# More feed-forward buffers, tail splits on GpSimd, and six other edits to a two-layer encoder step on one core

## The chip, the cores and the metric

The kernel runs on one core of a Trainium2 chip. The metric is the time of one execution on the device in microseconds, the median of several runs. The engines go by the profile's names: PE is TensorE (matmuls; PEld are its weight loads), DVE is VectorE, ACT is ScalarE, POOL is GpSimd, and SP is SyncE, which here only issues DMAs.

## The reference, cut to what matters

One step of a two-layer encoder (`D_MODEL` 1024, feed-forward width 2816) for 1024 prompt frames and 32 sample frames, in float32. Layer 0 mixes with a matrix-memory recurrence over 8 heads, layer 1 with windowed attention. Each mixer and each feed-forward is followed by a layer norm.

```python
def swiglu(x, w_gu, w_down):
    g, u = jnp.split(x @ w_gu, 2, axis=-1)
    return (jax.nn.silu(g) * u) @ w_down

def mlstm_chunk(q, k, v, ig, lf, C0, n0, m0):
    ...
    qk = jnp.einsum('bhtd,bhsd->bhts', q, k) * d
    num = w_inter[..., None] * jnp.einsum('bhtd,bhde->bhte', q, C0) + jnp.einsum('bhts,bhse->bhte', qk, v)
    ...
    C_new = decay[..., None, None] * C0 + jnp.einsum('bhs,bhsd,bhse->bhde', w_end, k, v)

def trunk(x, ...):
    for layer in range(DEPTH):
        ...  # mix: recurrence with w_in_a, w_out_a, or attention with w_kv, w_q_b, w_out_b
        x = layer_norm(DEEPNORM_ALPHA * x + mix, ln_g[layer, 0], ln_b[layer, 0])
        x = layer_norm(DEEPNORM_ALPHA * x + swiglu(x, w_gu[layer], w_down[layer]), ln_g[layer, 1], ln_b[layer, 1])
```

Outputs are the two sets of frames, the recurrence's states and the last keys and values.

## The kernel before

**Data and splits.** Prompt and sample frames stand side by side as 1056 columns; the 1024 features lie in 8 tiles of 128 partitions. Every large matmul is made from three matmuls in a reduced float format: each operand is split into a high half (a cast on ACT) and a low half (the difference), and `gemm` (L361 to L363) adds high x high, high x low and low x high. The activations' halves are the tile `SX`, made by `split_act` (ACT L391, DVE L392).

**Weights.** The class `Weights` brings 512 KB pieces from memory into three raw buffers (`wr`) and makes their halves in order, two jobs for a unit: the cast on ACT (L201), the low half on POOL, or on DVE for keys in `on_vector` (both L203). Five slots (`wh`, `wl`) hold the products; some jobs have a home of their own elsewhere (`W.home`, shown as `ex`, `oh`). Down projections of pairs use sums and differences of weight quarters (seven products instead of eight, L174 to L180 on DVE). A raw buffer is loaded anew when its last job is done.

**Order.** The order of instructions is fixed while the program is built. `gemm` calls `wv.tick` with the estimated PE time after each step, and `Weave` then lets background tasks (norms, staging of feed-forward results, feeding of loads) issue their next piece. Engines run their queues in order, so an instruction that waits holds those behind it.

**Stages.** First q, k, v of the recurrence: frames in three column groups, head pairs j = 0 to 3. The recurrence runs as a background pipeline per pair and chunk of 128 frames; chunk c = 8 is the sample, with 32 rows, and its tiles are cut to `[:L]`. `scores`, `values` and `place` hold its matmuls (L886 to L953). Then the mixer's output and its norm by quarters of 264 columns, and the feed-forward: `up_tile` makes hidden tiles with PSUM tags `A` and `B` of two buffers each; results lie in `Z` buffers from the list `free` (six of eleven), and `stage` splits pairs of them through buffers 7 to 10 and stores them (L1269 to L1271). `alloc` drains the oldest staging task when `free` is empty. The last tile runs `behind` after each product, which loads blocks for the down projection. `down` adds into `act` (L1465, L1467).

**Tail.** The last block of the down projection runs by quarters and output tiles (eight units, L1520 to L1525), with five PSUM banks in a ring, and after each quarter a norm task `ln_task`. The very last quarter of the kernel has a class of its own, `LastNorm`, which sums while the products come and ends with the variance, the scaling and the stores (L549 to L587).

```python
            if final and g == 3:
                wv.drain(tasks[1])
                run(g, cols, None, LastNorm(box[0].z, box[0].lnps, QUARTERS[g], li))
```

## Time and profile before

| | |
|---|---|
| median of 3 runs | 2239.36 us (2236.99 to 2242.18) |
| the profiled execution | 2235.46 us, span 2233.7 us |
| granted TensorE clock | 0.996 |
| busy: PE, DVE, ACT, POOL | 2184.5, 1465.8, 998.1, 1035.1 us |
| moved by DMA | 298.10 MB |

The span runs from the first to the last instruction of the profiled execution. A row of the timeline gives the start in us, the length in us, the engine, the line of the kernel, the operation, what it writes and reads, its shape and count, and in brackets the engine's idle time before it and what ended it. Two matmuls in a row overlap, so their lengths add up to more than the time that they hold PE; starts are what counts.

### The profile page before, as it was taken

The numbers are of one execution on the slowest core, as the hardware profiler recorded it, in microseconds if no ns is written. First come the engines' busy times: TensorE is split into PE (matmuls) and PEld (weight loads), VectorE is DVE, ScalarE is ACT, GpSimd is POOL, SyncE is SP. The second block draws the span as 40 slices with busy tenths as digits, with TensorE's granted clock in tenths as the row PEclk, the third lists the DMA queues.
The fourth block names the chain that finished last, engine by engine and source line by source line (L and its number), as shares of the span: only waits on it lengthen the run. The fifth ranks groups of instructions, "written<-read, shape, count | busy, mean of one in ns | idle before, by whom it ended". The sixth has DMA issues, their size and how long they took to land.

```text
span 2233.7 us, 44246 instructions
## 1 busy us (share of the span) xinstructions
PE 2184.5 (98%) x17086; PEld 2147.9 (96%) x17086; DVE 1465.8 (66%) x2848; ACT 998.1 (45%) x2253; POOL 1035.1 (46%) x977
## 2 busy tenths in 40 slices
PE   9999999999999999999999999999999999999997
PEld 9899989999999999999998999899999999999997
DVE  4465577777566565566667778788565666456657
ACT  4443355455444444322236778756444444332124
POOL 2544331003666666544316776600566666554422
PEclk9999999999999999999999999999999999999998
DMA  4222112211433443697426433411344434397712
GB/s 150 74 55 67 48 44 87 98 39 58 164 137 143 154 145 143 217 331 237 159 78 179 114 99 96 152 65 39 116 152 158 143 130 152 135 353 240 256 50 79
DMA packets 174499, 298.10 MB, mean 133 GB/s; under 512 B 18064, under 2 KB 130760, under 8 KB 174288
## 3 DMA queue, kind: packets, MB, share of 16 engines
q1 hardware_dynamic: 169936, 290.94, 39.0%
q10 hardware_dynamic: 4352, 4.33, 0.6%
q8 instruction: 135, 2.21, 0.4%
q14 instruction: 76, 0.62, 0.1%
HBM read 201.80 MB, written 82.94 MB: 127 GB/s over the span
## 4 chain that ended last, share of the span: by engine, by line
PE 77%; DVE 9%; ACT 5%; DMA 3%; issue 3%; POOL 2%; SPq 0%; ACTq 0%; POOLq 0%; DVEq 0%
PE A L361 9%; PE A L363 9%; PE A L362 9%; PE d L361 8%; PE d L363 8%; PE d L362 8%; PE B L361 7%; PE B L362 7%; PE B L363 7%; PE T L1737 1%; ACT act L463 1%; POOL wl L203 1%; DMA sx<-hs_t 1%; DMA wr<-in_dn 1%; PE O L1752 1%
## 5 line engine op out<-in xcount | busy, mean ns | idle before, releaser
L203 POOL TENSOR_TENSOR wl_s<-wr,wh_s 128x512 fp32r<-128x512 f32 x224 | 316.4, 1432 | 242.9 <-ACT wh_s L201 178.3
L361 PE MATMUL d<-sx,wh 128*128 128x264 f32 (+2 forms) x1068 | 340.5, 319 | 0.7 <-DVE act L1525 0.7
L363 PE MATMUL d<-sx,wl 128*128 128x264 f32 (+2 forms) x1068 | 325.5, 305 | 1.4 <-POOL wl L203 1.4
L362 PE MATMUL d<-sx,wh 128*128 128x264 f32 (+2 forms) x1068 | 324.9, 304 | 0.4 <-DVE sx L392 0.4
L203 POOL TENSOR_TENSOR wl_a<-wr,wh_a 128x512 fp32r<-128x512 f32 x112 | 169.1, 1516 | 324.8 <-ACT wh_a L201 204.8
L201 ACT CAST wh_s<-wr 128x512 fp32r<-128x512 f32 x224 | 135.4, 617 | 310.3 <-DVE wr L178 282.7
L361 PE MATMUL A<-sx,wh_s 128*128 128x264 f32 x896 | 254.7, 284 | 3.2 <-ACT z L1358 3.2
L362 PE MATMUL A<-sx,wh_s 128*128 128x264 f32 x896 | 254.2, 284 | 0.0
L363 PE MATMUL A<-sx,wl_s 128*128 128x264 f32 x896 | 254.0, 284 | 0.0
L361 PEld LDWEIGHTS d<-sx,wh 128*128 128x128 f32 x1068 | 201.8, 189 | 4.1 <-ACT z L444 1.1
L363 PEld LDWEIGHTS d<-sx,wl 128*128 128x128 f32 x1068 | 201.4, 189 | 2.4 <-POOL wl L203 2.0
L362 PEld LDWEIGHTS d<-sx,wh 128*128 128x128 f32 x1068 | 201.8, 189 | 1.5 <-DVE sx L392 0.7
L203 POOL TENSOR_TENSOR wl<-wr,wh 128x512 fp32r<-128x512 f32 (+2 forms) x91 | 120.6, 1335 | 176.1 <-ACT wh L201 153.2
L361 PE MATMUL d<-sx,ex 128*128 128x264 f32 x624 | 180.6, 289 | 0.4 <-ACT sx L391 0.2
L363 PE MATMUL d<-sx,ex 128*128 128x264 f32 x624 | 177.6, 285 | 3.2 <-DVE ex L203 3.2
L362 PE MATMUL d<-sx,ex 128*128 128x264 f32 x624 | 177.3, 284 | 0.2 <-DVE sx L392 0.2
L361 PEld LDWEIGHTS A<-sx,wh_s 128*128 128x128 f32 x896 | 168.4, 188 | 3.6 <-ACT z L1358 3.6
L363 PEld LDWEIGHTS A<-sx,wl_s 128*128 128x128 f32 x896 | 168.8, 188 | 0.0
L362 PEld LDWEIGHTS A<-sx,wh_s 128*128 128x128 f32 x896 | 168.4, 188 | 0.0
L1270 POOL TENSOR_TENSOR z<-z 128x528 fp32r<-128x528 f32 x76 | 105.1, 1383 | 108.0 <-issue 56.0
L1717 POOL TENSOR_SCALAR s<-s,st 128x256 f32<-128x256 f32 (+1 forms) x144 | 123.0, 866 | 43.9 <-DVE st L1715 28.7
L1269 ACT CAST z<-z 128x528 fp32r<-128x528 f32 x136 | 85.9, 631 | 96.1 <-DVE z L1282 46.1
(338 smaller groups left out, 7288.7 us busy)
## 6 DMA issues: line engine op xcount, KB each, us to landing
wr<-in_gu SPq DMA_DIRECT2D x92, 512.0 KB, 4.9
hs_x<-z SPq DMA_DIRECT2D x72, 528.0 KB, 2.8
hs_t<-z SPq DMA_DIRECT2D x64, 528.0 KB, 2.9
sx<-hs_x SPq DMA_DIRECT2D x112, 264.0 KB, 5.8
sx<-hs_t SPq DMA_DIRECT2D x64, 264.0 KB, 6.6
ex<-hs_t SPq DMA_DIRECT2D x64, 264.0 KB, 6.4
wr<-in_dn SPq DMA_DIRECT2D x32, 512.0 KB, 4.3
ex<-hs_x SPq DMA_DIRECT2D x32, 264.0 KB, 6.5
```

Of the source, the lines that this page charges most:

```text
L201: self.nc.scalar.copy(hi, r)
L203: eng.tensor_sub(lo, r, hi.bitcast(F32))
L361: nc.tensor.matmul(out, ah, bh, start=start and k == 0, stop=False, **kw)
L362: nc.tensor.matmul(out, ah, bl, start=False, stop=False, **kw)
L363: nc.tensor.matmul(out, al, bh, start=False, stop=stop and k == last, **kw)
L463: nc.scalar.activation(z, z, AF.Identity, scale=gk, bias=bk)
L1269: nc.scalar.copy(hi.bitcast(F32R), buf(s))
L1270: eng.tensor_sub(lo.bitcast(F32R), buf(s), hi)
L1717: nc.gpsimd.tensor_scalar_mul(p[:R, h, lo:256], p[:R, h, lo:256], st[:R, 2, h : h + 1])
L1737: nc.tensor.transpose(pt[:nk, i, h, :R], p[:R, h, c : c + nk], ident[:R, :R])
L1752: nc.tensor.matmul(po[:, :, :R], v, s["hi"][:nk, i, :, :R], start=(i == 0), stop=False)
```

## The change

Eight edits, none of which changes what is computed. `load_to` can load a weight in two halves, and the first weight's halves are interleaved with input tiles. All low halves of the last down block are made on POOL (before, the second one of each unit on DVE), and three low halves of the first weights on DVE (before, two). The recurrence's sample chunk uses whole 128-row tiles, padded with zeros that POOL writes. `Z` has two more buffers, both in `free`. The last `up_tile` issues its last Silu before it goes on to the next weight and the loads. The ring of five banks is turned by three. `LN_LAG` gets an entry for quarter 2 of the first feed-forward norm. In the last norms POOL's share of quarter 2's scaling goes to DVE and ACT, and `LastNorm.end` has another order.

```diff
-LN_LAG = {(2, 0): 7.0}
+LN_LAG = {(1, 2): 1.0, (2, 0): 7.0}
...
-    def load_to(self, i):
+    def load_to(self, i, between=None):
...
+            self.nc.sync.dma_start(r[:, : w // 2], ap[:, : w // 2])
+            between()
+            self.nc.sync.dma_start(r[:, w // 2 : w], ap[:, w // 2 :])
...
-        on_vector.update((u, 1) for u in dn[TAIL])
...
-    on_vector.update((u, f) for u in U_Q[:1] for f in range(2))
+    on_vector.update([(0, 0), (0, 1), (1, 0)])
...
             if s < n:
-                eng = nc.gpsimd if rush and s & 1 else nc.vector
-                eng.tensor_mul(z2(s), z2(s), rs.unsqueeze(1).broadcast_to([P, 2, w]))
+                nc.vector.tensor_mul(z2(s), z2(s), rs.unsqueeze(1).broadcast_to([P, 2, w]))
...
-                    if rush and k & 1:
-                        nc.gpsimd.tensor_scalar(z, z, gk, bk, op0=ALU.mult, op1=ALU.add)
-                    elif li & 1 and last and k & 1:
+                    if li & 1 and last and k & 1:
...
             nc.tensor.matmul(pm, onesm[:], acc, start=True, stop=False)
+            nc.tensor.matmul(pm, onesm[:], self.z(last - 1), start=False, stop=False)
             nc.tensor.matmul(pv, onesm[:], q, start=True, stop=False)
-            nc.tensor.matmul(pm, onesm[:], self.z(last - 1), start=False, stop=False)
...
-            shift(0)
             nc.vector.scalar_tensor_tensor(var, pv, eps_ln[:], d2, op0=ALU.add, op1=ALU.subtract)
...
-            for p in range(1, KT // 2):
+            for p in range(3):
                 shift(p)
...
                 z2 = self.z(2 * p, 2)
+                if p == 3:
+                    shift(p)
                 nc.vector.tensor_mul(z2, z2, rs.unsqueeze(1).broadcast_to([P, 2, self.w]))
...
-                    if k & 1:
+                    if k & 1 and p > 1:
...
-            W.load_to(0)
-            for k in range(KT):
-                nc.sync.dma_start(act[k][g][:], A["x"][:, k, t0 : t0 + n])
-            W.load_to(1)
+            W.load_to(0, lambda: inputs(0, 1))
+            inputs(*range(2, KT))
+            W.load_to(1, lambda: None)
...
-    W.split_to(0)
+    W.factor(0, 0)
...
+            if (g, k) == (0, 1):
+                W.split_to(0)
...
-        kT[j] = new(pa, "kT", [P, T], bufs=2)
+        kT[j] = new(pa, "kT", [P, SEQ + P], bufs=2)
+        nc.gpsimd.memset(kT[j][:, T:], 0.0)
+        nc.gpsimd.memset(vt[j][:, 8], 0.0)
...
+    wide = {tag: pa.tile([P, 2, n], F32, name=tag) for tag, n in (("p8", P), ("k8", DK), ("h8", DV))}
+    for t in wide.values():
+        nc.gpsimd.memset(t[:], 0.0)
...
-                nc.tensor.matmul(ph[:L, h, :], s["p"][:L, h, :L], vt[j][:L, c, h, :], start=True, stop=C is None)
+                nc.tensor.matmul(ph[:, h, :], s["p"][:, h, :], vt[j][:, c, h, :], start=True, stop=C is None)
...
-            self.z = new(self.zx.enter_context(pool("z", side="right")), "z", [P, 11, 2, N4])
+            self.z = new(self.zx.enter_context(pool("z", side="right")), "z", [P, 13, 2, N4])
...
-        free = list(range(6))
+        free = [*range(6), 11, 12]
...
-            mul(a, "s4", "x22", again=True)
...
+            def gate1():
+                nc.scalar.activation(buf(s1), a, AF.Silu)
+
+            mul(a, "s4", "x22", behind and gate1, again=True)
...
             def rest():
-                nc.scalar.activation(buf(s1), a, AF.Silu)
+                if not behind:
+                    gate1()
...
         dense_psum(5)
+        for _ in range(3):
+            psbank()
```

`mul` runs its new argument `then` behind its matmuls and ahead of `W.done` and `behind`. The score, key and transposing matmuls of the sample chunk change as the one shown.

More of the change, by code (lines that the diff above doesn't have):

```diff
@@ L159, in load_to @@
             r = self.pool.tile([P, WD], F32, name=f"wr{u}", tag="wr", bufs=RAW)
-            self.nc.sync.dma_start(r[:, :w], ap)
             self.raw[u] = r
             self.nload += 1
+            if between is None:
+                self.nc.sync.dma_start(r[:, :w], ap)
+                continue
+            self.nc.sync.dma_start(r[:, : w // 2], ap[:, : w // 2])
+            between()
+            self.nc.sync.dma_start(r[:, w // 2 : w], ap[:, w // 2 :])
     def _source(self, u, f):
@@ L631, with inputs @@
         if g == 0:
-            W.load_to(0)
-            for k in range(KT):
-                nc.sync.dma_start(act[k][g][:], A["x"][:, k, t0 : t0 + n])
-            W.load_to(1)
+            def inputs(*ks):
+                for k in ks:
+                    nc.sync.dma_start(act[k][0][:], A["x"][:, k, : GRP[0][1]])
+            W.load_to(0, lambda: inputs(0, 1))
+            inputs(*range(2, KT))
+            W.load_to(1, lambda: None)
         else:
@@ L885, in scores @@
             ps = new(psa, "S", [P, 2, P])
-            nc.tensor.matmul(ps[:L, :, :L], kT[j][:, c0 : c0 + L], s["q"][:, :, :L], start=True, stop=True)
+            nc.tensor.matmul(ps[:, :, :L], kT[j][:, c0 : c0 + P], s["q"][:, :, :L], start=True, stop=True)
             pt = new(psa, "T", [P, 512], bufs=2)
-            nc.tensor.transpose(pt[:L, :P], kT[j][:, c0 : c0 + L], ident[:])
-            s["p"] = new(pa2, "p", [P, 2, P], bufs=2)
+            nc.tensor.transpose(pt[:, :P], kT[j][:, c0 : c0 + P], ident[:])
+            s["p"] = new(pa2, "p", [P, 2, P], bufs=2) if c < 8 else wide["p8"]
             nc.vector.tensor_mul(s["p"][:L, :, :L], ps[:L, :, :L], s["d"][:L, :, :L])
-            s["k"] = new(pa2, "ks", [P, 2, DK], bufs=2)
+            s["k"] = new(pa2, "ks", [P, 2, DK], bufs=2) if c < 8 else wide["k8"]
             we = cols[g][:L, c % 3, 32 + 2 * j : 34 + 2 * j].unsqueeze(2).broadcast_to([L, 2, DK])
@@ L901, in values @@
             for h in range(2):
-                nc.tensor.matmul(ph[:L, h, :], s["p"][:L, h, :L], vt[j][:L, c, h, :], start=True, stop=C is None)
+                nc.tensor.matmul(ph[:, h, :], s["p"][:, h, :], vt[j][:, c, h, :], start=True, stop=C is None)
                 if C is not None:
-                    nc.tensor.matmul(ph[:L, h, :], s["qw"][:, h, :L], C[:], start=False, stop=True)
-            keys = s["k"][:L].rearrange("p h d -> p (h d)")
-            nc.tensor.matmul(pc[:, : 2 * (DV + 1)], keys, vt[j][:L, c], start=True, stop=True)
+                    nc.tensor.matmul(ph[:, h, :], s["qw"][:, h, :], C[:], start=False, stop=True)
+            keys = s["k"][:].rearrange("p h d -> p (h d)")
+            nc.tensor.matmul(pc[:, : 2 * (DV + 1)], keys, vt[j][:, c], start=True, stop=True)
             small = new(pa2, "small", [P, 5, 2], bufs=3)
@@ L944, in values @@
             nc.vector.tensor_mul(u, u, rr)
-            s["h"] = new(pa2, "ht", [P, 2, DV], bufs=2)
+            s["h"] = new(pa2, "ht", [P, 2, DV], bufs=2) if c < 8 else wide["h8"]
             nc.vector.tensor_mul(s["h"][:L], ph[:L, :, :DV], u.unsqueeze(2).broadcast_to([L, 2, DV]))
@@ L952, in place @@
             for h in range(2):
-                nc.tensor.transpose(pt[:, h * P : h * P + L], s["h"][:L, h, :], ident[:L, :L])
+                nc.tensor.transpose(pt[:, h * P : (h + 1) * P], s["h"][:, h, :], ident[:])
             nc.scalar.copy(act[2 * j][g][:, off : off + L], pt[:, :L])
@@ L1324, in up_tile, with mul @@
             u = up[i]
-            def mul(ps, f, o, **kw):
+            def mul(ps, f, o, then=None, **kw):
                 w = tiles_of(W.factor(u, f))
@@ L1331, in mul @@
                     gemm(ps[:, c, :], w, tiles(X[o](c)), **kw)
+                if then:
+                    then()
                 W.done(u, f)
```

## The prediction

> **What bounds the kernel now.** I read the page first, then the waits of TensorE (PE), then the timeline at each of them. The page:

> ```profile
> span 2233.7 us, 44246 instructions
> ...
> PE 2184.5 (98%) x17086; PEld 2147.9 (96%) x17086; DVE 1465.8 (66%) x2848; ACT 998.1 (45%) x2253; POOL 1035.1 (46%) x977
> ```

> TensorE is busy for 98% of the span, so 2233.7 - 2184.5 = 49.2 us are all that better overlap can give without taking matmuls away. Each microsecond won has to be one in which PE waits, one before its first matmul, or one behind its last. The view of waits, PE alone, gives their owners (total us, times, longest):

> ```profile
> PE A L361 <- ACT z L1358: 3.2, 2, 2.0
> PE d L363 <- DVE ex L203: 3.2, 5, 1.1
> ...
> PE A L361 <- ACT z L1370: 2.1, 2, 1.7
> ...
> PE ln L438 <- DVE z L434: 2.1, 2, 1.1
> PE ln L555 <- DVE z L544: 2.1, 1, 2.1
> ...
> PE A L361 <- DVE act L1465: 0.8, 1, 0.8
> PE d L361 <- DVE act L1525: 0.7, 1, 0.7
> ```

> All edits but two aim at a row of this list. Nearly every wait is short and stands alone, so the question for each is what comes late next once it is gone.

> **First loads.** Half of weight 0 comes first, then two input tiles, then the other half; only the first half is split ahead of the inputs, and the first half of weight 1 is split on VectorE (DVE). Three rows of the start:

> ```profile
> 6.09 3.85 DVE L392 TENSOR_TENSOR sx<-act,sx 128x384 fp32r<-128x384 f32 x8
> 6.69 0.44 PE L362 MATMUL d<-sx,wh 128*128 128x384 f32 x1 [0.42 <-DVE sx L392]
> 12.07 0.44 PE L363 MATMUL d<-sx,wl 128*128 128x384 f32 x1 [0.74 <-POOL wl L203]
> ```

> The second matmul waits 0.42 us since DVE makes both halves of the weight before it touches an input. At 12.07 PE waits 0.74 us for GpSimd (POOL), while DVE, free after 6.09 + 3.85 = 9.94, could have made that half. Both waits go: 1.16 us. PE may also start earlier, as the first half of a transfer lands before the whole; but it takes an input tile each 3.85 / 8 = 0.48 us, as DVE does, and the last tile lands no sooner (as many bytes ahead of it, and SyncE issues more transfers). I take 1.4 us, between 0.4 (the inputs pace the start, and part of the second wait stays) and 2.2.

> **Whole tiles for the sample chunk.** Its matmuls had 32 rows or 32 columns. PE at one group of value matmuls of a prompt chunk, then of the sample chunk:

> ```profile
> 121.99 0.38 PE L902 MATMUL H<-vt,p 128*128 128x129 f32 x2
> ...
> 123.13 0.47 PE L361 MATMUL d<-wh,sx 128*128 128x256 f32 x1
> ```

> ```profile
> 131.55 0.40 PE L902 MATMUL H<-vt,p 32*32 32x129 f32 x2
> ...
> 133.52 0.33 PE L710 MATMUL d<-wh,xs 128*64 128x256 f32 x1
> ```

> The same ten instructions hold PE for 123.13 - 121.99 = 1.14 us as whole tiles, and for 133.52 - 131.55 = 1.97 us as part tiles. Four head pairs: 4 x 0.83 = 3.3 us off PE itself, with no wait involved. The score and placing matmuls change form too; no row shows a 64-wide one on whole tiles, so I allow 0.5 us either way, and 1 us less where DVE, not PE, sets the chain. I take 2.8, between 1.5 and 3.8. The price is zeroing on POOL: three buffers once, two strips per pair, eleven fills:

> ```profile
> 21.02 0.81 POOL L838 MEMSET qz<- 128x256 f32 x3
> ```

> At 0.27 us each they make 3 us in all, under 1.4 of it at the start, where POOL next has a weight half to make. Behind the strips in POOL's queue are weight halves and the masking for the recurrence; the ones that stand there already wait for the same old readers. I cost them at nothing; without cover they are 3 us.

> **Two more feed-forward buffers.** The 3.2 us at L1358 (2.0 and 1.2, once in each layer) have their cause on ScalarE (ACT):

> ```profile
> 570.36 0.63 ACT L1269 CAST z<-z 128x528 fp32r<-128x528 f32 x1 [4.66 <-DMA hs_t<-z]
> 571.82 0.60 ACT L1358 COPY z<-A 128x528 f32<-128x528 f32 x1 [0.83 <-DVE z L1270]
> ```

> `alloc` finds no buffer, drains the staging task, and so puts its L1269, which waits for a store to land, ahead of L1358, which empties the bank PE needs. With eight buffers `alloc` finds one. Staging then runs at its own pace, 5.2 us a step; the risk is that its end meets the next pair's start in the same four staging buffers, with the same wait a tile later. I take 3.2, between 0 and 3.4.

> **Silu of the last tile.** `gate1` goes ahead of the next weight split on ACT. Now it stands behind it, in layer 1:

> ```profile
> 1976.71 0.62 ACT L201 CAST wh_s<-wr 128x512 fp32r<-128x512 f32 x1 [3.43 <-DVE wr L178]
> 1977.24 0.60 ACT L1370 ACTIVATE z<-A 128x528 f32<-128x528 f32 x1
> ```

> PE waits 2.1 us for it over both layers. What is late next: some 19 us on, a weight pair that lands late holds DVE, behind it L1465, which empties a bank:

> ```profile
> 1996.05 0.70 DVE L1465 SCALAR_TENSOR_TENSOR act<-act,A 128x528 f32<-128x528 f32 x1
> ```

> In layer 0 PE already waits 0.8 us there; in layer 1 it was just in time. That pair comes with its transfer, not with PE, so most of the 2.1 is given back. I take 0.8, between 0 and 2.1.

> **Tail splits on POOL.** 3.2 us, five times, for low halves that DVE makes:

> ```profile
> 1110.19 0.43 DVE L1525 TENSOR_TENSOR act<-act,d 128x264 f32<-128x264 f32 x1 [1.00 <-PE d L363]
> 1110.54 0.55 DVE L203 TENSOR_TENSOR ex<-wr,ex 128x384 fp32r<-128x384 f32 x1
> 1112.39 0.43 DVE L1525 TENSOR_TENSOR act<-act,d 128x264 f32<-128x264 f32 x1 [1.30 <-PE d L363]
> ...
> 1122.76 1.43 DVE L601 TENSOR_TENSOR z<-z,act 128x528 f32<-128x528 f32 x1
> ```

> ```profile
> 1122.61 1.01 POOL L203 TENSOR_TENSOR ex<-wr,ex 128x384 fp32r<-128x384 f32 x1 [1.95 <-ACT ex L201]
> ```

> Each DVE split stands behind L1525, which waits for PE to end a tile, and sometimes behind L601; so it is born late. On POOL it waits for its cast alone. POOL then has 2 x 1.01 = 2.02 us for each unit, while PE takes 1112.39 - 1110.19 = 2.20. It fits by 0.18, and four halves are made ahead; raw buffers also come free sooner. I take the whole 3.2, between -5 (below) and 4.

> [...]

> **Lag and turned ring.** `LN_LAG` puts the variance matmul of quarter 2 of the first feed-forward norm 1.0 us of PE work later; L438 waited 1.0 there (2.1 in two places; the other, of quarter 3, stays). The ring of five banks is turned by three, so the first product of the keys no longer takes the bank that L1525 has yet to read: 0.7. The unused tiles issue nothing. I take 1.7, between 0.5 and 2.1.

> **Last norm.** The end of the kernel, DVE and then POOL:

> ```profile
> 2217.56 1.41 DVE L544 TENSOR_TENSOR z<-z 128x264 f32<-128x264 f32 x1
> 2218.89 0.42 DVE L558 TENSOR_TENSOR act<-act,d 128x264 f32<-128x264 f32 x1
> 2222.09 0.70 DVE L566 TENSOR_TENSOR act<-act,ln 128x528 f32<-128x528 f32 x1 [2.78 <-ACT z L562]
> 2222.72 0.48 DVE L569 SCALAR_TENSOR_TENSOR z<-ln,eps_ln,z 128x264 f32<-128x264 f32 x1
> 2223.12 1.92 DVE L566 TENSOR_TENSOR act<-act,ln 128x528 f32<-128x528 f32 x3
> ```

> ```profile
> 2216.89 1.79 POOL L453 TENSOR_TENSOR act<-act,z 128x528 f32<-128x528 f32 x1
> ```

> L544 takes 1.41 us beside a POOL operation where L558, as large, takes 0.42. Without POOL its two L453 come to DVE (2 x 0.64 = 1.3, by the row of three), while L544 gives back 1.0 and the two-input operations before it an amount that no row here isolates, which I bound by the same 1.0: -0.3 to 0.7 earlier, and I take 0.7, since POOL is busy beside them all. ACT takes four more affine steps. PE's two matmuls L556 leave the chain behind L544: 0.45 by my estimate. The variance step goes ahead of a shift of 0.64, but its sum may not be there before, so 0.2 to 0.6, and I take 0.5; the loop loses two affine steps of 0.42 and gains a shift of 0.64: 0.2. Together 1.9, between 0 and 2.6.

> **Sum.** 1.4 + 2.8 + 3.2 + 0.8 + 3.2 + 1.7 + 1.9 = 15.0 us. Against the profiled execution, 2235.46 us with its span of 2233.7, that is 2220.5; its time is below all three runs shown, so I take the sum from their median: 2239.36 - 15.0 = 2224.4. About 0.2% (4.5 us) is what a measurement of this kernel tells from no change.

> **The rivals.** *The waits come back further on* (0.24): the start is paced by inputs (0.4 instead of 1.4), the staging wait moves a tile on (0), the Silu's gain is returned (0), the last norm gives half (0.9). Left: 0.4 + 2.8 + 3.2 + 1.7 + 0.9 = 9.0, so 2230.4. For it speaks the L1465 row, late or just in time; against it that the list names no other wait of that size in the stretches between.

> *GpSimd bounds the tail* (0.06, slower): if each split is held once by a two-input DVE operation, it takes 1.01 + 0.70 = 1.71 us, 3.42 a unit against PE's 2.20. Eight units and two layers lose 16 x 1.22 = 19.5 us; the other terms bring 11.8, so 2239.4 + 7.7 = 2247.1. It decides from the point where 16 x (2s - 2.20) passes 11.8: splits of s = 1.47 us. Against it: DVE has such an operation only behind every second product. [...]

> *The change doesn't do what it says* (0.08): buffers run out still, PE's part-tile cost sits in what surrounds the sample chunk, and a new wait or two eats the rest; 12 of 15 us lost give 2236.4.

> **How the numbers follow.** Forecast 0.62. It and the first rival are faster by over 0.2%: 0.86; the third is within it: 0.08; the second slower: 0.06. The range goes from 2217, where every term is near its upper end or the runs sit as low as the profiled one, to 2235, which takes in the first rival and its lower terms.

> **What would show it.** Right: in the waits of PE the rows at L1358, L1370, `ex` L203 and L1525 gone; the value matmuls of the sample chunk near 1.14 us a group; the splits of the tail on POOL near 1.0 us; L544 near 0.42. Wrong: a new wait on POOL `ex` in the tails, a wait for ACT one tile after 572, a longer L1465 wait, or a start where PE waits for inputs.

## The result, and the profile after

The changed kernel took 2231.05 us (median of 6 runs, 2230.43 to 2233.30) where the kernel before took 2238.18: a ratio of 0.997, interval 0.9957 to 0.9982, or 7 us. A second set of 5 runs gave 2227.94 us and 0.9954 (0.994 to 0.9968), 10 us. So it is faster, by 0.3% and 0.5%, and both times lie inside the predicted range. But the gain is just under half of the 15.0 us of the forecast in the first set, and two thirds of it in the second. The first rival's 2230.4 came nearest.

The page, two lines, and then the waits of PE (total us, times, longest) that answer to those of before:

```profile
span 2231.5 us, 44260 instructions
...
PE 2184.5 (98%) x17086; PEld 2154.7 (97%) x17086; DVE 1452.1 (65%) x2833; ACT 1000.8 (45%) x2259; POOL 1042.2 (47%) x997
```

```profile
PE A L365 <- DVE act L1485: 3.3, 2, 1.7
PE ln L442 <- DVE z L438: 2.8, 1, 2.8
PE d L365 <- DVE act L1547: 2.4, 1, 2.4
PE d L365 <- ACT qT L697: 1.8, 1, 1.8
PE A L365 <- ACT z L1366: 1.7, 2, 1.3
...
PE ln L557 <- DVE z L545: 0.4, 1, 0.4
```

The lines of the code have moved: L361 is now L365, L203 L208, L434 L438, L438 L442, L544 L545, L1358 L1366, L1465 L1485, L1525 L1547. The five waits for `ex` and the two for the Silu are gone, and the last norm's wait fell from 2.1 to 0.4. In their place stand a new wait of 1.8 us at the start, and three old ones that grew: L1485 (0.8 before), L438 (1.1 there before) and L1547 (0.7 before).

Sums of waits do not say where time is kept. For that I took the start of each of the 15,568 matmuls into the tiles `d`, `A` and `B` in one trace, less the start of the same matmul in the first profile of before. The table gives how this difference moves in each stretch of before's clock (us; minus is a gain). "Again" is a second profile of the kernel before, and shows how far two executions of one program differ. The stretch from 60 to 125, where nothing moves by more than 0.4, is left out.

| stretch | what lies there | forecast | before again | changed, 1st | changed, 2nd | splits alone | tiles + norm alone | buffers + Silu alone | loads + lag alone |
|---|---|---|---|---|---|---|---|---|---|
| 0-60 | first loads | -1.4 | +0.6 | +2.1 | +1.5 | +0.5 | +0.8 | +0.2 | +1.5 |
| 125-450 | sample tiles | -2.8 | 0.0 | -2.8 | -2.8 | 0.0 | -2.9 | +0.2 | 0.0 |
| 450-800 | buffers, layer 0 | -3.2 with layer 1 | +0.7 | -0.7 | -0.5 | -0.9 | -0.7 | -0.8 | -0.5 |
| 800-1100 | Silu, layer 0 | -0.8 with layer 1 | -0.1 | +0.4 | +0.2 | 0.0 | +0.1 | +2.1 | +0.5 |
| 1100-1178 | tail, layer 0 | -3.2 with layer 1 | +0.1 | -2.6 | -2.6 | -2.6 | -0.4 | -0.3 | +0.2 |
| 1178-1219 | lag, ring | -1.7 | -0.3 | +4.0 | +2.6 | +2.2 | +2.3 | +0.3 | +2.5 |
| 1219-1580 | nothing changed | 0 | +0.2 | +2.7 | +0.3 | -0.5 | 0.0 | -0.2 | +1.5 |
| 1580-1800 | buffers, layer 1 | above | +0.2 | -0.8 | -0.7 | -0.1 | -0.3 | -0.8 | -0.2 |
| 1800-2130 | Silu, layer 1 | above | +0.2 | 0.0 | +0.2 | +0.9 | 0.0 | -0.3 | -0.1 |
| 2130-2157 | tail, layer 1 | above | +0.7 | -2.0 | -2.0 | -2.0 | +0.1 | +0.8 | +0.1 |
| 2157-end | last norm | -1.9 | -0.6 | -2.6 | -2.5 | -0.6 | -2.4 | +0.3 | -0.7 |

Sample tiles, tails and last norm show in every profile that holds them, and only there. First loads and lag cost.

### The profile page after: what moved, and what is told of

Read it like the earlier page. It is cut to its first block, busy times and chain, and to the rows that moved or that the text cites. A ratio compares the mean times of both kernels' runs of the same rounds, so it can differ in the third digit from the quotient of the medians.

```text
span 2231.5 us, 44260 instructions
## 1 busy us (share of the span) xinstructions
PE 2184.5 (98%) x17086; PEld 2154.7 (97%) x17086; DVE 1452.1 (65%) x2833; ACT 1000.8 (45%) x2259; POOL 1042.2 (47%) x997
## 4 chain that ended last, share of the span: by engine, by line
PE 60%; DVE 5%; DMA 3%; ACT 3%; issue 2%; POOL 2%; SPq 0%; POOLq 0%; DVEq 0%; ACTq 0%
PE A L365 9%; PE A L367 9%; PE A L366 9%; PE B L365 6%; PE B L366 6%; PE B L367 6%; PE d L365 4%; PE d L367 4%; PE d L366 4%; DMA wr<-in_dn 1%; PE T L1759 1%; ACT act L464 1%; POOL s L1739 1%; PE O L1774 1%; PE O L1775 1%
## 5 line engine op out<-in xcount | busy, mean ns | idle before, releaser
L208 POOL TENSOR_TENSOR wl_s<-wr,wh_s 128x512 fp32r<-128x512 f32 x224 | 316.1, 1430 | 247.2 <-ACT wh_s L206 189.6
L365 PE MATMUL d<-sx,wh 128*128 128x264 f32 (+2 forms) x1068 | 343.4, 322 | 4.6 <-DVE act L1547 2.4
L208 POOL TENSOR_TENSOR wl_a<-wr,wh_a 128x512 fp32r<-128x512 f32 x112 | 168.3, 1510 | 327.7 <-ACT wh_a L206 325.6
L365 PE MATMUL A<-sx,wh_s 128*128 128x264 f32 x896 | 254.9, 284 | 1.7 <-ACT z L1366 1.7
L365 PEld LDWEIGHTS d<-sx,wh 128*128 128x128 f32 x1068 | 203.3, 190 | 8.3 <-issue 2.6
L208 POOL TENSOR_TENSOR wl<-wr,wh 128x512 fp32r<-128x512 f32 (+2 forms) x94 | 123.1, 1318 | 177.1 <-ACT wh L206 174.5
L365 PE MATMUL d<-sx,ex 128*128 128x264 f32 x624 | 180.6, 289 | 0.4 <-ACT sx L395 0.2
L365 PEld LDWEIGHTS A<-sx,wh_s 128*128 128x128 f32 x896 | 168.4, 188 | 2.4 <-ACT z L1366 2.1
```

What stands on the lines that cost most here:

```text
L208: eng.tensor_sub(lo, r, hi.bitcast(F32))
L365: nc.tensor.matmul(out, ah, bh, start=start and k == 0, stop=False, **kw)
```

## Experiments: the change in four pieces

Each piece is one or two parts of the change, put into the kernel before.

**Low halves of the tail on POOL, alone**

```diff
-        on_vector.update((u, 1) for u in dn[TAIL])
```

> The kernel before with one edit of the change alone: the low halves of the two tails are made on GpSimd. Theory A (the tails' waits are a loss of their own): the five waits for these halves go, TensorE is 2.6 us earlier behind the first tail (1107 to 1130) and 2.0 behind the second (2140 to 2157), no wait grows in return, and the time falls by 4 to 5 us against the kernel before. Theory B (the norm behind the first tail takes its part back: it is bound by VectorE's chain): the gain of the first tail is lost again between 1178 and 1219, and 2 to 2.5 us are left. A third outcome, GpSimd as the bound (splits over 1.47 us, slower), is the prediction's second rival.

Measured: 2234.32 us, ratio 0.9978 (0.9968 to 0.9987), so 5.0 us by the medians. POOL's splits last 1.07 us with 24 of them, where the 12 of before lasted 1.05:

```profile
L203 POOL TENSOR_TENSOR ex<-wr,ex 128x384 fp32r<-128x384 f32 x24 | 24.5, 1069 | 0.7 <-ACT ex L201 0.6
```

2.6 us come in the first tail and 2.0 in the second. The time speaks for theory A; but the trace has theory B's loss too, 2.2 us between 1178 and 1219 where no line was changed. PE comes there 3.4 us earlier than in the first profile of before, and meets weights that are not yet split. The waits of PE in this version (before has 1.4 us in the first row, its second profile below 2.4, and neither has the second row):

```profile
PE d L362 <- POOL wl L203: 2.7, 3, 1.3
...
PE d L360 <- ACT wh L201: 1.1, 2, 0.9
```

These waits do not explain the loss. Between the same matmuls, those of 1178 to 1219, PE idles 5.1 us here and 5.5 in the second profile of before, which loses nothing there. The difference is the granted clock, which the profile gives as a share of full speed. Between 1200 and 1209 it is 0.62 here and 1.00 in the second profile of before. A row gives the window, its length, the busy times of PE, PEld, DVE, ACT and POOL with their instructions, the granted clock, the DMA share and GB/s:

```profile
1200.00:1209.00 9.00, 7.97 (x28) 7.28 (x29) 5.51 (x8) 3.15 (x8) 5.69 (x5) 0.62 0.56 163
```

```profile
1200.00:1209.00 9.00, 6.82 (x37) 6.14 (x37) 6.26 (x9) 6.06 (x13) 6.73 (x6) 1.00 0.51 150
```

The experiments on the clock, below, show what brings this about.

**Sample tiles and last norm, alone** (all of their edits, such as)

```diff
-        kT[j] = new(pa, "kT", [P, T], bufs=2)
+        kT[j] = new(pa, "kT", [P, SEQ + P], bufs=2)
...
-            shift(0)
...
-                    if k & 1:
+                    if k & 1 and p > 1:
```

> The kernel before with two parts of the change alone, which lie far from each other: whole tiles for the sample chunk, and the reordered last norm without GpSimd. Theory A (both are off TensorE's path for good): between 125 and 450 us TensorE gains 2.9 us against the kernel before, as in all profiles of the changed kernel, behind 2216 us the span gains 2.5 us, and the time falls by 5 to 5.5 us. Theory B (the recurrence around the sample chunk is bound by VectorE, and TensorE's gain there only fills a loss made at the start by the changed kernel): below 1.5 us at the sample chunk when the start is the old one, 4 us or less in all.

Measured: 2232.92 us, 0.9977 (0.9967 to 0.9986), 5 us by the ratio and 6.4 by the medians. The table has 2.9 us at the sample tiles with the old start, so theory A holds and B falls. The same stretch 1178 to 1219 takes 2.3 us back here as well, again with a clock of 0.62 between 1200 and 1209.

**Buffers and Silu, alone**

```diff
-        free = list(range(6))
+        free = [*range(6), 11, 12]
...
-            mul(a, "s4", "x22", again=True)
+            mul(a, "s4", "x22", behind and gate1, again=True)
```

> The kernel before with two parts of the change alone: two more feed-forward buffers, and the Silu of a pair's last tile ahead of the next weight split. Theory A (their waits come back one tile later): TensorE gains 2.2 us at 572 and returns 1.3 to 1.5 at 585, gains 0.6 by 960 and 2.0 by 1990 and returns them at 964 and 2000, and keeps 1 to 2 us in all, a time of 2236 to 2238. Theory B (as predicted, 3.2 and 0.8): 4 us, about 2235.

Measured: 2237.28 us, 0.9992 (0.9983 to 1.0001): about 2 us, not told from nothing. The time is that of theory A. Two rows of this version's waits of PE show what came back:

```profile
PE A L361 <- DVE act L1472: 3.6, 2, 2.0
...
PE A L361 <- ACT z L1353: 1.5, 2, 1.1
```

The +2.1 between 800 and 1100 has its cause here too: the clock falls to 0.5 for 3.4 us from 965.2, right behind the wait of 2.0 us for L1472.

**First loads and lag, alone** (the new order of loads and splits, and)

```diff
-LN_LAG = {(2, 0): 7.0}
+LN_LAG = {(1, 2): 1.0, (2, 0): 7.0}
...
-            W.load_to(0)
+            W.load_to(0, lambda: inputs(0, 1))
```

> The kernel before with two parts of the change alone: the first loads, and the lag of 1.0 us (the ring stays, as the three unused tiles take no bank anyway). Theory A (both cost): 1.5 to 4 us later at 24 us, and 1 to 3 us lost between 1178 and 1219 beyond what the kernel before loses there; slower than before by 2 to 4 us, about 2241 to 2243. Theory B (as predicted, 1.4 and 1.0 gained): 2236 to 2237.

Measured: 2241.53 us, 1.0011 (1.0002 to 1.002): slower by 2.5 us, as theory A has it. Three of its waits of PE are those of the changed kernel:

```profile
PE ln L443 <- DVE z L439: 2.8, 1, 2.8
...
PE d L366 <- DVE act L1536: 2.4, 1, 2.4
...
PE d L366 <- ACT qT L698: 1.8, 1, 1.8
```

**Before, again** (no edit)

> The kernel before once more, unchanged, for a second profile of it. Both theories: 2234 to 2243 us, as its runs so far. Theory A (the first profile of before was a lucky execution between 1178 and 1219): TensorE loses 1.5 to 2.5 us there against the first profile, with a half clock near 1200 behind its waits, as in the two versions that differ from it only elsewhere. Theory B (the loss there comes with whatever makes TensorE earlier): the stretch is as in the first profile, within 0.5 us.

Measured: 2237.13 us, a single run. Theory B: PE loses nothing between 1178 and 1219, so the loss there belongs to versions in which PE comes over 3 us earlier or the lag stands. The first profile of before is not free of it: it has 3.4 us at half clock from 1186.1. By their ratios the four pieces make 4.9 + 5.1 + 1.8 - 2.5 = 9.3 us, and the change as a whole brought 7 to 10.

## Experiments: the start

ACT of the changed kernel ahead of its first query copy, and PE behind it:

```profile
17.04 4.76 ACT L395 CAST sx<-act 128x384 fp32r<-128x384 f32 x12 [1.97 <-DMA act<-in_x]
21.70 0.47 ACT L697 COPY qT<-d 128x384 f32<-128x384 f32 x1
```

```profile
22.23 0.44 PE L365 MATMUL d<-sx,wh 128*128 128x384 f32 x1 [1.82 <-ACT qT L697]
```

The copy that empties the first query bank stands behind all 24 casts of inputs, and these wait for transfers. In the trace of before the same copy came 2.1 us sooner and PE did not wait for it:

```profile
19.63 0.47 ACT L687 COPY qT<-d 128x384 f32<-128x384 f32 x1
```

**First loads as before, in the changed kernel**

```diff
-            W.load_to(0, lambda: inputs(0, 1))
-            inputs(*range(2, KT))
-            W.load_to(1, lambda: None)
+            W.load_to(0)
+            for k in range(KT):
+                nc.sync.dma_start(act[k][g][:], A["x"][:, k, t0 : t0 + n])
+            W.load_to(1)
...
-    W.factor(0, 0)
+    W.split_to(0)
```

> The changed kernel with the order of its first loads and splits as in the kernel before (weight 0 whole, eight input tiles, weight 1 whole, both halves of weight 0 split ahead of the inputs by VectorE). Theory A (the new order costs): two more transfers on SyncE's queue bring every later input 1.3 us later, ScalarE casts them in order and empties the first query bank behind them, so TensorE waits 1.8 us at 22; undone, that wait goes, TensorE is 2 us earlier from 24 us on, and the time falls by about 2 us, to about 2229. Theory B (the loss is caught up in the recurrence, where VectorE sets the pace): TensorE is earlier at 24 us, but no longer at 130 us, and the time is that of the changed kernel within 0.7 us.

Measured: 2228.64 us, 0.9954 (0.9942 to 0.9967). The wait at 22 is gone, as theory A has it, and PE is 1.0 us later than in the first profile of before at 60 us instead of 1.5 to 2.1. That gain stays through 1100, against theory B's story, but the time is no lower than the changed kernel's 2227.94. One execution differs from the next by as much as this part is worth, so the time leaves it open.

**Small loads later**: five small transfers move behind all inputs; the new order stays.

```diff
-        if g == 0:
-            gbias = pa.tile([40, 1], F32, name="gbias")
...
-            nc.sync.dma_start(ident[:], A["ident"])
+    gbias = pa.tile([40, 1], F32, name="gbias")
...
+    nc.sync.dma_start(ident[:], A["ident"])
     W.factor(0, 0)
```

> The changed kernel with its five small loads (two biases, a state, a mask, the identity) issued behind all input tiles and the first value weights instead of behind the first group's inputs; the new order of the first loads stays. Theory A (the loss at the start is one of SyncE's queue: every later input is issued later): the inputs of groups 1 and 2 are issued about 2.4 us sooner, ScalarE's casts with them, the wait of 1.8 us for the first query bank at 22 goes, and TensorE is 2 us earlier from 24 us on; the time falls by 1.5 to 2.5 us. Theory B (the loads are bound by their bytes, not by their issue): the inputs land when they did, the wait stays, and the time is the same within 0.7 us.

Measured: 2227.37 us, 0.9951 (0.9938 to 0.9964). SP and ACT of this version:

```profile
7.04 4.36 SPq L644 DMA_DIRECT2D act<-in_x  x8
```

```profile
18.66 0.47 ACT L696 COPY qT<-d 128x384 f32<-128x384 f32 x1
```

SP issues the later inputs from 7.04 instead of 9.69, the copy comes 3 us sooner, and PE stands at +0.2 at 60 us. So the mechanism of theory A is right: the loss is one of SP's queue. The time fell by 0.6 us, less than expected and within what runs differ by. Over all traces, PE stood at +1.5 to +4.0 at 60 us in the eight with the new order alone (mean 2.5), and at 0 to +1.0 in the seven with the old one (mean 0.5): the part costs 2.0 us by 60 us. No time of a run shows this cost by itself.

## Experiments: the lag and the ring

DVE and PE of the changed kernel, where PE waits 2.4 us:

```profile
1179.04 0.71 DVE L435 TENSOR_TENSOR z<-z 128x528 f32<-128x528 f32 x1 [1.18 <-POOL z L435]
1179.78 0.43 DVE L438 TENSOR_TENSOR z<-z 128x264 f32<-128x264 f32 x1
1180.13 0.42 DVE L1547 TENSOR_TENSOR act<-act,d 128x264 f32<-128x264 f32 x1
1180.59 0.71 DVE L603 TENSOR_TENSOR z<-z,act 128x528 f32<-128x528 f32 x1
1181.21 0.76 DVE L1547 TENSOR_TENSOR act<-act,d 128x264 f32<-128x264 f32 x2
```

```profile
1181.78 0.66 PE L365 MATMUL d<-sx,wh 128*128 128x384 f32 x1 [2.37 <-DVE act L1547]
```

The keys' first product waits for the sum of tile m = 6, the first of the two at 1181.21. In the built program m = 6 and the keys' first product have the same bank, in the changed kernel as in the one before. The three unused tiles take no bank, so **the ring was never turned**.

**No lag**

```diff
-LN_LAG = {(1, 2): 1.0, (2, 0): 7.0}
+LN_LAG = {(2, 0): 7.0}
```

> The changed kernel with its lag of 1.0 us for quarter 2 of the first feed-forward norm taken out again, nothing else. Theory A (the lag does harm): it moves the variance product of quarter 2 into the keys' first product, so the scaling of quarter 2 falls into the chain of quarter 3, which took 24.2 us from the last product's end to the end of its last sum (1179.5 to 1203.7), against 21.3 us before (1183.1 to 1204.4). Without the lag that chain is 21 to 22 us again, the wait of TensorE for the last sum of quarter 3 falls from 2.8 us to about 1, and the time falls by 2 to 3 us, to about 2228.5. Theory B (the chain is long because of what runs beside it, not of the lag): the wait of 1.0 us for quarter 2 comes back, the chain stays near 24 us, and the time is that of the changed kernel within 1 us (2230 to 2232).

Measured: 2227.78 us, 0.9953 (0.9939 to 0.9966). The stretch 1178 to 1219 stands at -0.2 instead of +2.6 and +4.0, and the wait for quarter 3's sum fell to 1.1: theory A's steps. The time is that of the changed kernel's second set; the start of the profiled execution was 1.8 us later (+3.3 at 60 us), which this edit does not touch.

**Ring truly turned**

```diff
-            psbank()
+            nc.vector.memset(psbank()[:, :1], 0.0)
```

> The changed kernel in which the three tiles taken to turn the ring of PSUM banks are written once each (one column, VectorE, some 60 ns each). In the built program of the changed kernel the three unused tiles take no bank: the keys' first product stands on the bank of product m = 6 of the last quarter, as in the kernel before. Written, they take banks, and the keys' first product stands on the bank of m = 3. Theory A (the chain of quarter 3 decides): the wait of 2.4 us ahead of the keys' first product goes, but VectorE gets to quarter 3 no sooner, so that the wait for the last sum of quarter 3 grows from 2.8 to about 5 us, and the time stays at 2231 within 1 us. Theory B: TensorE's 2.4 us are won, and the time falls by 2 us or more, to about 2228.5.

Measured: 2226.75 us, 0.9945 (0.9933 to 0.9958). PE passes from the last product of the tail to the keys' first without a wait:

```profile
1180.75 0.28 PE L367 MATMUL d<-sx,ex 128*128 128x264 f32 x1
1180.87 0.34 PE L365 MATMUL d<-sx,wh 128*128 128x384 f32 x1
```

Theory B holds: the stretch is at -0.7, in spite of +4.0 at the start. The time is 1.2 us below the changed kernel's second set. Theory A was wrong since quarter 3's norm begins with a product behind the keys' first (L426), so it moves up with it, from 1188.6 to 1186.2.

**No lag, ring turned, old loads**

> The changed kernel without the lag, with the ring truly turned (three tiles written once), and with its first loads as in the kernel before. Theory A (the three are separate): against the changed kernel minus 2 us at the start, minus 3 to 4 us between 1178 and 1219, 2225 to 2226, below each of the three alone. Theory B (lag and turn stand for each other: with the ring turned, the lag is what keeps the variance product out of the way): the wait of 1 us for the variance of quarter 2 comes back and is not hidden, so that it is not below the version with the lag and the turned ring (2226.8) by more than 0.5 us in spite of the better start.

Measured: 2227.01 us, 0.9947 (0.9934 to 0.996). The variance's wait of 1.0 us is back, and the stretch is at +1.7: theory B. So the lag is good only with the turn, as far as one trace with the turn alone shows. Without the turn, the lag puts the wait for DVE in front of the keys' product, where it is longer: seven traces with lag and no turn (the one of the failed filling below left out) lie at +1.3 to +4.0 (mean 2.8), six with neither at -0.3 to +2.3 (mean 0.7), three with both at -0.7 to 0.0.

## Experiment: the Silu

**Silu as before, in the changed kernel**

```diff
-            mul(a, "s4", "x22", behind and gate1, again=True)
+            mul(a, "s4", "x22", again=True)
...
-                if not behind:
-                    gate1()
+                gate1()
```

> The changed kernel with the Silu of a pair's last tile back behind the next weight split on ScalarE. Theory A (its gain is given back one tile later, where a weight pair comes with its transfer): TensorE waits for the Silu again, 2 us over both layers, the two waits for the emptied bank of the down product shrink from 3.3 us to about 1, and the time is that of the changed kernel within 0.7 us. Theory B (as predicted, part of it stays): slower by 0.8 to 2 us, 2232 to 2233.

Measured: 2229.36 us (2227.12 to 2231.4), 0.9956 (0.9943 to 0.9968). The time cannot tell, since the two sets of the changed kernel are 3.1 us apart. The stretches cannot either: +0.6 between 800 and 1100 and -0.2 between 1800 and 2130 lie among those of the other versions. The waits of PE can:

```profile
PE A L365 <- ACT z L1384: 2.5, 2, 1.6
...
PE A L365 <- DVE act L1484: 0.9, 1, 0.9
```

The Silu's wait is back, and the wait for the emptied bank is 0.9 instead of 3.3 us. Together they are 3.4 us, so the edit only moves the wait, as theory A has it. DVE of the changed kernel shows the pair that comes with its transfer, and the emptying held behind it:

```profile
962.48 0.69 DVE L179 TENSOR_TENSOR wr<-wr,wr 128x512 f32<-128x512 f32 x1 [0.38 <-DMA wr<-in_dn]
963.09 1.31 DVE L1485 SCALAR_TENSOR_TENSOR act<-act,A 128x528 f32<-128x528 f32 x2
```

## Experiments: the clock

Between 1219 and 1580 nothing was changed, yet the first trace of the changed kernel loses 2.7 us there, and the second 0.3. Busy times and the granted clock in two windows, of the first trace, the second, and the last experiment below:

```profile
1181.00:1185.00 4.00, 3.22 (x9) 3.04 (x10) 2.18 (x7) 0.04 (x1) 0.00 (x0) 0.59 0.30 89
1200.00:1209.00 9.00, 6.10 (x19) 5.61 (x20) 5.45 (x7) 3.25 (x7) 6.97 (x6) 0.62 0.52 157
```

```profile
1181.00:1185.00 4.00, 4.00 (x23) 3.93 (x23) 2.16 (x7) 1.33 (x3) 0.00 (x0) 1.00 0.19 62
1200.00:1209.00 9.00, 7.54 (x27) 7.36 (x28) 5.55 (x9) 3.27 (x7) 4.96 (x4) 0.62 0.60 143
```

```profile
1200.00:1209.00 9.00, 7.79 (x50) 7.20 (x49) 6.68 (x9) 4.67 (x10) 8.16 (x6) 1.00 0.51 148
```

**Changed kernel, again** (no edit)

> The changed kernel once more, unchanged, as the measure for the runs beside it. Both theories: 2230 to 2232 us, as measured. What the profile is for: in the first profile of the changed kernel the granted clock was 0.5 for 3.4 us from 1181.7, 6.8 us from 1202.2, 3.4 us from 1243.2 and 6.8 us from 1434.3. Theory A (the half clock follows a window of 3.41 us in which TensorE idled for some 1.4 us or more, and the windows lie anew in each execution): the stretches at 1182 and 1202, behind idle times of 2.4 and 2.8 us, come back in most executions; those at 1243 and 1434, behind shorter ones, may not. Theory B (nothing to do with idle time): they lie elsewhere.

Measured: 2227.94 us, below what was expected. The half clock behind the wait of 2.8 us came again, the ones at 1182, 1243 and 1434 did not. The first profile has the figures of theory A: its shorter stretches last 3.413 us, and the least idle time in such a window ahead of one is 1.44 us. What came again is as theory A has it but for one point: a half clock behind the 2.4 us at 1182 does not come back in most executions. Of the six other traces with this wait, this one among them, two have it.

**Two waits filled**

```diff
+        if g == 0:
+            for _ in range(9):
+                nc.tensor.matmul(psS[0][:, :P], onesm[:], onesm[:], start=True, stop=True)
         ps = project(U_KV[g > 0][0], g)
```

and ten such products ahead of the last sum of quarter 3.

> The changed kernel with products that nobody reads in two of TensorE's waits: nine of 128x128 (0.22 us each at full clock) ahead of the keys' first product, ten ahead of the last sum of quarter 3. They leave the waits' ends where they are. Theory A (TensorE's idle time lowers the granted clock afterwards): no half clock near 1182 and 1203, the slow products there (0.65 us instead of 0.38) are gone, and from 1178 to 1219 TensorE loses 1.5 to 2.5 us less than the 4.0 us against the kernel before that the changed kernel lost; the time falls by 1 to 2 us. Theory B (the clock falls for another reason): the half clock stays there and the time is the same within 0.5 us, or up to 1 us longer where the products outlast a wait.

Measured: 2234.32 us, 0.9986 (0.9977 to 0.9995): 6 us slower than the changed kernel. The first filling failed: its products waited 3.9 us for DVE's write to their bank, 6.4 us lost between 1178 and 1219, and a half clock followed that idle time. At 1203, with the wait filled, there was none.

**One wait filled** (the ten products alone)

> The changed kernel with ten products that nobody reads (128x128, 0.22 us each) ahead of the last sum of quarter 3 alone, where TensorE waits 2.8 us; the filling of the other wait is left out, since there the products themselves waited 3.9 us for a write of VectorE to their bank. Theory A (idle time lowers the clock afterwards): no half clock from 1202 on, where every profile with that wait unfilled had one, and from 1198 to 1219 TensorE loses 1 to 1.5 us less; the time falls by 0.5 to 1.5 us. Theory B: half clock there all the same, no gain.

Measured: 2229.93 us, 0.9967 (0.9955 to 0.9978). PE behind quarter 3's sum, in the changed kernel's second trace and in this one:

```profile
1202.80 0.53 PE L366 MATMUL d<-sx,wh 128*128 128x384 f32 x1
1203.12 0.53 PE L367 MATMUL d<-sx,wl 128*128 128x384 f32 x1
```

```profile
1205.85 0.34 PE L366 MATMUL d<-sx,wh 128*128 128x384 f32 x1
1206.03 0.34 PE L367 MATMUL d<-sx,wl 128*128 128x384 f32 x1
```

With the wait filled the products last 0.34 us instead of 0.53, and the window above has a clock of 1.00 instead of 0.62. The half clock followed the unfilled wait of 2.8 us in all eight traces that have it, and the filled one in neither of two. The mechanism of theory A is shown. A wait of 2.8 us is not the only way there: of the eight traces with 1.0 to 1.1 us at this place, four have a half clock at 1200 too. The gain is about 1 us (PE loses 2.6 us between 1198 and 1219, where seven of the eight unfilled traces lose 3.5 to 3.7), and it is not seen in the time.

## Experiments: two repairs together

**Ring turned and small loads later**, and the same **with the old order of first loads**

> The changed kernel, lag kept, with two repairs together: the ring of PSUM banks truly turned (three tiles written once), and the five small loads behind all input tiles. Theory A (the two add up): 2 us at the start and 3 us between 1178 and 1219 against the changed kernel, so about 2223 to 2224.5, below every kernel so far. Theory B (what the start wins is waited for later): not below the version with the turned ring alone (2226.8) by more than 0.7 us.

> The changed kernel with its lag, the ring truly turned, the five small loads behind all input tiles, and the first loads in the order of the kernel before. Theory A (the new order of the first loads costs also where the small loads are out of the way): TensorE earlier at 24 us than with the new order and the small loads later (-0.3 to -0.5 us against before), and the time at or below 2225.2. Theory B (with the small loads out of the way the new order is as good): the same time within 0.7 us.

Measured: 2225.16 us, 0.9947 (0.9935 to 0.996), and 2225.73 us, 0.9941 (0.9927 to 0.9954). By the medians both are below the changed kernel in either set, by 2 to 6 us, and 13 to 14 us below before. By the ratios they are clear of its first set (0.997), not of its second (0.9954). Against the turned ring alone (2226.75) the small loads bring 1.6 us by the medians and nothing by the ratios, 0.9947 against 0.9945, so the first one's theories stay undecided. Its trace has both gains, +0.5 at 60 us and -0.1 between 1178 and 1219, but also 2.4 us lost between 800 and 1100, with a half clock from 964.7 behind a wait of 2.3 us for L1484. Of the second one's theories, B holds: +1.2 at 60 us is no better than the +0.5 of the new order, and the times agree.

## Where the prediction was right, and which steps failed

The sum failed in four of its seven terms. First loads, buffers, Silu, and lag with ring were forecast at 7.1 us together and cost about 3. The other three, forecast at 7.9, brought 9.7.

**First loads: wrong in sign.** Forecast a gain of 1.4, found a loss of 2.0 by 60 us. The step that failed is "the last tile lands no sooner (as many bytes ahead of it, and SyncE issues more transfers)": I named the extra transfers and priced them at nothing for the inputs behind them. SP issued the later inputs from 9.69 us instead of 8.34, ACT's casts of them came later too, and the copy behind these casts, which had been just in time at 19.63 us, came at 21.70. I had checked what is late next within the first 12 us only.

**Sample tiles: right.** 2.9 us for 2.8. A group of value and key matmuls took what its whole-tile twin takes, 134.89 - 133.75 = 1.14 us:

```profile
133.75 0.39 PE L915 MATMUL H<-vt,p 128*128 128x129 f32 x2
...
134.89 0.47 PE L720 MATMUL d<-wh,xs 128*64 128x256 f32 x1
```

**Buffers: the risk came true.** I took 3.2 and named the risk that staging's end meets the next pair's start, "with the same wait a tile later". ACT of the changed kernel at that place, then PE waits 1.3 us for L1366:

```profile
581.54 0.63 ACT L1282 CAST z<-z 128x528 fp32r<-128x528 f32 x1 [3.65 <-issue]
...
583.98 0.63 ACT L1282 CAST z<-z 128x528 fp32r<-128x528 f32 x1 [0.74 <-DMA hs_t<-z]
...
585.03 0.59 ACT L1366 COPY z<-A 128x528 f32<-128x528 f32 x1
```

1.5 us are left against the first profile of before, 0.8 of it in layer 1. In layer 0, three versions without this edit moved by -0.5 to -0.9 too (before again by +0.7), so there it may have brought nothing. I count it at 1. The step that failed is the size: "I take 3.2", near the upper end, for a wait that mostly moved.

**Silu: zero instead of 0.8.** The mechanism was named, and all of the gain was returned, not "most": 3.4 us of waits with the old order, 3.3 with the new.

**Tails: mis-sized, too low.** 4.6 instead of 3.2. I priced the idle time before the five matmuls that wait for `ex` (0.18, 0.40, 1.12, 0.40 and 1.06 us). What follows each of them starts 0.44, 0.67, 1.38, 0.67 and 1.32 us earlier once it is gone, 0.26 or 0.27 more each. A matmul behind a wait overlaps none before it: it lasts 0.39 us and the next starts 0.23 behind it, where 0.28 and 0.12 are usual. PE before the change:

```profile
1118.93 0.39 PE L363 MATMUL d<-sx,ex 128*128 128x264 f32 x1 [0.40 <-DVE ex L203]
1119.16 0.28 PE L361 MATMUL d<-sx,ex 128*128 128x264 f32 x1
1119.28 0.29 PE L362 MATMUL d<-sx,ex 128*128 128x264 f32 x1
```

POOL did not bound the tails: its splits last 1.06 us on average in the changed kernel and 1.07 in the piece alone, far from the 1.47 at which the second rival decides. No run shows that rival's 1.71 us for a split, nor a loss like the -5 at which the range of this term began. In the changed kernel the one split of each tail that starts during an L603 takes 1.49 or 1.50 us, and the other 22 take 1.00 to 1.03. The L601 of 1122.76 before the change, beside a split, took 1.43 us, where the L603 of the same form that meets no split, at 1120.67 in the changed kernel, takes 0.71. Two such meetings in 24 splits are too few to matter.

**Lag and ring: wrong in sign.** Forecast a gain of 1.7, found a loss of about 2. The step that failed is "the first product of the keys no longer takes the bank that L1525 has yet to read". I took three tiles that nothing writes for a turn of the ring, though I had written myself that "the unused tiles issue nothing". The lag's own step failed too. I priced the one wait that it removes, and not what then comes late on DVE: without the lag the keys' first product waits 0.7 us and quarter 3's sum 1.1, with it 2.4 and 2.8.

**Last norm: right.** 2.5 us against the first profile, some 2.2 against the mean of the five traces without the edit; forecast 1.9. The 0.45 us of the two L556 can be read in the first profile of before, where they start at 2219.57 and the next product at 2220.02. L545 runs at the short length:

```profile
2218.12 0.43 DVE L545 TENSOR_TENSOR z<-z 128x264 f32<-128x264 f32 x1
```

**Sum.** -2.0 + 2.9 + 1 + 0 + 4.6 - 2 + 2.2 = 6.7, where 7 to 10 were measured; two sets of one kernel differ by as much as the rest. What I left out altogether is the clock: idle time is paid twice where the clock falls behind it (to 0.62 between 1200 and 1209), and the stretch 1178 to 1219 takes up to 2.3 us in this way from a PE that comes early. The first rival had the right kind of story and, by errors that cancel, almost the right time, which is luck: it kept the lag's 1.7 and a gain at the start, both of which were losses.

## What to carry to other kernels

Price a removed wait by what is late next, and follow it through the queues that the edit lengthens: here, with two more transfers at the head of SP's queue, the later inputs were issued 1.35 us later, the copy that empties a bank, behind the casts of these inputs on ACT, came 2.1 us later, and PE waited 1.8 us for it. Check a rotation of buffers in the addresses of the built program: the three tiles here that nothing wrote took no bank. With effects of 1 to 3 us in executions that differ by as much, take a second profile of the old kernel and compare stretch by stretch, at the starts of the same instructions and with the granted clock beside them.
